# Six columns of attention's output projection run inside attention, with other banks and low parts around the scan and the FFN entries

## The chip, the cores and the metric

The kernel runs on one core of a Trainium2 chip. The metric is the device time of one execution in microseconds (us): the median of the runs.

## The reference

One step of a two-layer streaming encoder on 1024 prompt rows and 64 sample rows, D = 1024, all in float32. Layer 0 is a Mamba-2 scan with a SwiGLU FFN, layer 1 a banded attention with another.

```python
# layer 0
zxbcdt = rmsnorm(x) @ ssm_w_in          # z, x|B|C, dt
xbc = silu(conv4(x|B|C));  dt = softplus(dt + bias)
y, state = ssd_scan(xbc, dt, -exp(A_log), B, C, h0)    # chunks of 64, 32 heads of 64, 4 groups, state 128
y = rmsnorm_per_group((y + xs * D) * silu(z)) @ ssm_w_out
x = x + rmsnorm(y)
x = x + rmsnorm((silu(u @ w_g) * (u @ w_u)) @ w_out)   # u = rmsnorm(x); hidden 2816
# layer 1: K, V from x; q from rmsnorm(x); 16 heads of 64, 9 chunks of 64 keys, clipped relative bias
x = x + rmsnorm(band_attention(q, K, V) @ attn_w_o)
x = x + FFN(x)                                          # as above
```

## The kernel before

Everything is held transposed, features on the 128 partitions and rows on the free axis. The 1088 rows are cut in three slices `SL` (384, 384, 320) for the scan and attention, and in four quarters `QS` (256, 256, 288, 288) for the projections and FFNs. A float32 product is made of three passes: a matrix is split in a rounded high part and a low part (value minus high part), and `passes` issues high x high, high x low, low x high for each of the 8 blocks of 128 features. `unit` takes a PSUM bank, calls `passes` (24 matmuls) and evacuates the result. The third of each three matmuls is the only reader of a weight's low part.

`Weights` streams the weights through rings: SyncE loads one 128 x 1024 tile into a `raw` buffer, `part` casts it on ScalarE into a slot of the ring `hl` (or `hx`), and VectorE subtracts for the low part (line 341). For a weight planned with `acc` the low part is made otherwise: ScalarE writes the negated high part (335), and a DMA issued by GpSimd (336) loads the weight again from DRAM and adds it. A plan lists all weights in the order of use; a slot is taken again when the weight in it is given back with `W.put`. In the FFN's later part two weights are combined into sums (`pair`: ta, tb, half) for a Strassen scheme: `run_pair`. The first `NB0` = 6 hidden blocks run as plain products (`plain_pairs`, results in tiles `x`, PSUM tiles `mmx`), each with a gate and a mult weight, while VectorE and ScalarE build the sums of the activations (`op_build`, lines 1141 to 1174) that the first `run_pair` (tiles `px`) needs. `NACC` = 3 of the six are loaded with `acc`.

A `Stream` sets the order of the program: each `unit` advances a clock by the planned length of its matmuls, and side tasks (generators: norms, scan steps, attention blocks) are woken by that clock with waits from tables such as `TB_V`. Each engine then runs its own instructions in that order, with few exceptions where a priority is raised.

In the scan, `table_task` makes the running sum of the decay (`acsp`, copied to `nac`, line 696), `ssd_task` transposes (`xtp`, 866), multiplies (`xd`, `xe`) and makes states (`sp`, 885) and outputs (`yp`, 816). The norm's sums (`nst`, 487) and its broadcast (`nbp`, 517) take banks from `ax`: the pool `pax` has two banks, shared with xtp and sp; `pyy` has four, for yp.

In attention, heads go in pairs j = 0 to 7. `att_task` makes scores (S, 1681), transposes (ptp, 1712) and po (1747); a pair's result goes to DRAM (`oscr`) and `build_o` loads it back as split tiles `r`, with the last pair taken from SBUF. `uo[q]` is set when quarter q has all of them. Three columns (m = 0, 1, 2) of quarter 0's output projection run before attention's end; the rest in `start_att` by `project`, by groups `MGS` of weights.

Of the kernel before, what the change touches and what calls it, by code (L numbers as in the profile page):

```python
# [46 lines left out]
ST_W, ST_RB = (6.5, 22.0, 22.0), (6.0, 1.0, 1.0)  # L47
TB_W, TB_V = 1.0, 14.0
ES = 0.5, 0.5, 0.0
# [325 lines left out]
def hybrid_kernel(  # L375
# [57 lines left out]
    def col(c):  # L433
        return pcs[:, c:c + 1]

    def ax(name):
        return pax.tile([P, 512], F32, tag="ax", name=name)

# [129 lines left out]
    W.plan(*[dict(src=[w_in[t]]) for t in (32, 36, 16)])  # L568
    for grp in order:
        W.plan(*[dict(src=[w_in[{"B": 32, "C": 36, "x": 16, "z": 0}[kd_] + i]]) for kd_, i in grp])  # L570

# [31 lines left out]

    def project(qs, uq, y, src, after=None, early=None, pl=None):


        ss = {}
        for mg in MGS:
            ws = early if early and mg is MGS[0] else [W.get() for _ in mg]
            for q in qs:  # L610
                n = QS[q][1]
                st.wait_for(lambda: q in uq)
                for m, w_ in zip(mg, ws):
                    ym = y[q][m // 4][:, m % 4, :]

                    def ev(ps):
                        with tc.high_priority(HIP):
                            if src is None:
                                A.copy(ym, ps[:, :n])
                            else:  # L620
                                V.tensor_tensor(ym, src[q][m // 4][:, m % 4, :], ps[:, :n], op=ALU.add)

                    if not (ws is early and q == qs[0]):
                        unit(w_, uq[q], n, ev, pl=pl)
                    if after:
                        if m == 0:
                            ss[q] = ssum_start(n)
                        add_sq(ss[q], ym, n, m == 0)
                    if q == qs[-1]:
                        W.put()  # L630
# [7 lines left out]
    with ExitStack() as es:  # L638
# [413 lines left out]
        for s in range(NSL):  # L1052
# [24 lines left out]
            pend[s] = [dps] * (s < 2) + box  # L1077
        finish(2)
        for grp in order:
            ws = [W.get() for _ in grp]  # L1080
# [27 lines left out]
        project((0, 1), uy[0], ya, None)  # L1108
        st.wait_for(lambda: so["D"] == 3 * XT and len(rst_done) == NG * NSL)


# [116 lines left out]
    def ffn_plan(layer):  # L1228
        w1, w2 = w_f1[layer], w_f2[layer]
        W.plan(*[dict(src=[w1[i]], acc=t_ < NACC) for t_ in range(NB0) for i in (t_, FT + t_)])  # L1230
        for t_ in [*range(NB0, FT), *range(NB0)]:
# [8 lines left out]
    def plain_pairs(ts, ops, hd, px, tmp):  # L1240

        n = ops.n
        ws = [(W.get(), W.get()) for t_ in ts]
        for q in range(2):
            st.wait_for(lambda: all(a_ in ops.plain for a_ in (f"a{q + 1}1", f"a{q + 1}2")))
            uq = ops.plain[f"a{q + 1}1"] + ops.plain[f"a{q + 1}2"]
            for t_, w2 in zip(ts, ws):
                x = tmp.tile([P, n], F32, tag=("p1", "u3")[q] + f"{t_ % 2}", name="x")

                def gate(ps):  # L1250
                    with tc.high_priority(HIP):
                        A.activation(x, ps[:, :n], AF.Silu)

                def mult(ps):
                    with tc.high_priority(HIP):
                        V.tensor_tensor(x, ps[:, :n], x, op=ALU.mult)
                    nc.sync.dma_start(hd[:, t_, q * n:(q + 1) * n], x)

                for w, e in zip(w2, (gate, mult)):
                    unit(w, uq, n, e, pl=px)  # L1260
                    if q:
                        W.put()

# [270 lines left out]
    for j in range(2, 8):  # L1534
        W.plan(W_K[j], W_V[j], W_Q[j])
    for b in range(2):
        W.plan(*[dict(src=[w_o[m]]) for mg in MGS for m in mg])
    ffn_plan(1)
    done = done2
    uo = {}  # L1540
    with ExitStack() as es:
# [230 lines left out]
        def build_o():  # L1772

            for q, (o, n) in enumerate(QS):
                got = []
                of = ((0,), (0, 1), (1, 2), (2,))[q]
                for kh in range(2):
# [8 lines left out]
                    got += [(h[:, k, :], l_[:, k, :]) for k in range(4)]  # L1786
                if nk == 3:
                    yield 0, 0, lambda: all((7, s) in att_done for s in of)
                    for s in of:
                        a, b = max(o, SL[s][0]), min(o + n, SL[s][0] + SL[s][1])  # L1790
                        src = last_o[s][:, a - SL[s][0]:b - SL[s][0]]
                        with tc.high_priority(HIP):
                            A.copy(h[:, 3, a - o:b - o], src)
                            V.tensor_tensor(l_[:, 3, a - o:b - o], src, h[:, 3, a - o:b - o], op=ALU.subtract)
                uo[q] = got

# [77 lines left out]

        st.wait_for(lambda: 0 in uo and R.free())
        y0 = v4(R.get(), QS[0][1])
        wo = [W.get() for _ in MGS[0]]
        for m, w in enumerate(wo):
            unit(w, uo[0], QS[0][1], lambda p_: A.copy(y0[:, m, :], p_[:, :QS[0][1]]), parts=4)
        st.wait_for(lambda: cur["C"] == 8 * NCH and 1 in uo)  # L1880
# [4 lines left out]
    def start_att(ops, px, after, dn):  # L1885
        st.wait_for(lambda: RX.free(4))
        y = ops[0].y
        for q in range(2):
            y[q] = [v4(RX.get(), QS[q][1]) for _ in range(2)]
        G.tensor_copy(y[0][0][:, :3, :], y0[:, :3, :])  # L1890
        project((0, 1), uo, y, None, lambda q, ss: after(q, y[q], ss), early=wo, pl=px)
        R.put()
        st.spawn(op_build(ops[0], dn))
# [106 lines left out]
```

## Time and profile before

| what | before |
|---|---|
| median of 3 runs | 2969.83 us (2967.94 to 2970.08) |
| profiled execution | 2970.8 us, span 2969.1 us |
| mean granted TensorE clock | 0.996 |
| busy: PE, DVE, ACT, POOL | 2916.9, 2037.2, 1394.6, 723.7 us |
| HBM read, written | 292.47, 62.74 MB |

The profile is of one execution. Its times are in us from the span's start. A group's row ends in its busy time, the mean of one in ns, and the idle time of its engine just before it with the instruction that ended most of that. PE is TensorE, DVE VectorE, ACT ScalarE, POOL GpSimd, SP SyncE. Instruction rows of the timeline give start, length, engine, line, operation, tiles and, in brackets, idle time before it and who ended it.

### The profile page before, as it was taken

To read this page: it belongs to the slowest core of one execution; us is meant where nothing else is said; L and a number is where in the kernel's file an instruction comes from. 1 tells how busy PE (TensorE), PEld (TensorE's weight loads), DVE (VectorE), ACT (ScalarE), POOL (GpSimd) and SP (SyncE) were. 2 spreads that over 40 slices of the span, in tenths; PEclk is the share of its full clock that TensorE was granted. 3 is DMA by queue.
4 is the path that set the end of the run, shared out by engine and by line. 5 is a ranking of instruction groups with operands and counts; after the bars stand their busy time and mean duration, and the time that the engine had idled before them with its cause. 6 is when DMAs were issued, how large, how long until landed. Compare 5 with 4: busy or idle time off the path is not lost.

```text
span 2969.1 us, 56218 instructions
## 1 busy us (share of the span) xinstructions
PE 2916.9 (98%) x21562; PEld 2871.9 (97%) x21562; DVE 2037.2 (69%) x4455; ACT 1394.6 (47%) x2522; POOL 723.7 (24%) x877
## 2 busy tenths in 40 slices
PE   8999999999999999999999999999999999999999
PEld 7899999999999999999999899999899999999999
DVE  7887888785768555584557878778678645475544
ACT  6564645454454222244545666556653322244443
POOL 1333333331121343451111000000131333351111
PEclk9999999999999999999999999999999999999999
DMA  3333323234564222255655322223365222245654
GB/s 123 113 106 96 104 90 110 93 118 150 172 172 129 79 76 84 73 161 175 208 175 169 96 75 78 66 67 99 110 186 171 79 79 77 78 156 171 220 174 137
DMA packets 201550, 363.35 MB, mean 122 GB/s; under 512 B 20544, under 2 KB 149280, under 8 KB 201280
## 3 DMA queue, kind: packets, MB, share of 16 engines
q1 hardware_dynamic: 199488, 353.39, 38.3%
q0 software_dynamic: 1792, 6.36, 1.1%
q8 instruction: 169, 2.77, 0.4%
q14 instruction: 101, 0.83, 0.1%
HBM read 292.47 MB, written 62.74 MB: 120 GB/s over the span
## 4 chain that ended last, share of the span: by engine, by line
PE 85%; DVE 8%; DMA 3%; ACT 2%; issue 2%; POOL 0%; SPq 0%; DVEq 0%; ACTq 0%; POOLq 0%
PE px L1280 9%; PE px L1281 9%; PE px L1282 9%; PE mm L454 7%; PE mm L456 7%; PE mm L455 7%; PE po L1480 6%; PE po L1481 6%; PE po L1479 6%; PE mmx L455 3%; PE mmx L454 3%; PE mmx L456 3%; PE ptp L1712 2%; PE po L1747 2%; PE yp L816 1%
## 5 line engine op out<-in xcount | busy, mean ns | idle before, releaser
L454 PE MATMUL mm<-r,hl 128*128 128x384 f32 (+2 forms) x1664 | 555.1, 334 | 6.1 <-ACT BT L768 3.0
L456 PE MATMUL mm<-r,hl 128*128 128x384 f32 (+2 forms) x1664 | 539.6, 324 | 3.6 <-DVE hl L353 2.9
L455 PE MATMUL mm<-r,hl 128*128 128x384 f32 (+2 forms) x1664 | 538.2, 323 | 0.0
L341 DVE TENSOR_TENSOR hl<-raw,hl 128x1024 fp32r<-128x1024 f32 (+1 forms) x219 | 257.2, 1175 | 226.8 <-ACT hl L340 220.7
L1281 PE MATMUL px<-r,hl 128*128 128x288 f32 (+1 forms) x1184 | 347.3, 293 | 0.0
L454 PEld LDWEIGHTS mm<-r,hl 128*128 128x128 f32 x1664 | 315.4, 190 | 9.0 <-ACT BT L768 3.2
L456 PEld LDWEIGHTS mm<-r,hl 128*128 128x128 f32 x1664 | 314.5, 189 | 5.7 <-DVE hl L353 4.5
L455 PEld LDWEIGHTS mm<-r,hl 128*128 128x128 f32 x1664 | 315.3, 190 | 0.3
L1280 PE MATMUL px<-r,hl 128*128 128x288 f32 x1056 | 311.0, 294 | 0.0
L1282 PE MATMUL px<-r,hl 128*128 128x288 f32 x1056 | 310.7, 294 | 0.0
L340 ACT CAST hl<-raw 128x1024 fp32r<-128x1024 f32 (+1 forms) x219 | 220.0, 1005 | 175.3 <-PE po L1481 101.6
L480 POOL TENSOR_TENSOR ssum<-ssum,sq 128x256 f32<-128x256 f32 (+3 forms) x97 | 127.8, 1318 | 637.3 <-ACT sq L479 622.0
L1281 PEld LDWEIGHTS px<-r,hl 128*128 128x128 f32 x1184 | 222.3, 188 | 0.0
L1282 PE MATMUL px<-rx,hl 128*128 128x256 f32 x768 | 214.8, 280 | 6.7 <-DVE hl L341 6.7
L1280 PE MATMUL px<-rx,hl 128*128 128x256 f32 x768 | 215.3, 280 | 0.7 <-ACT hl L340 0.7
L1480 PE MATMUL po<-rx,hl 128*128 128x384 f32 (+1 forms) x624 | 201.7, 323 | 0.1
L1280 PEld LDWEIGHTS px<-r,hl 128*128 128x128 f32 x1056 | 198.4, 188 | 0.4 <-DVE u L1295 0.3
L1282 PEld LDWEIGHTS px<-r,hl 128*128 128x128 f32 x1056 | 198.3, 188 | 0.0
L1479 PE MATMUL po<-rx,hl 128*128 128x384 f32 (+1 forms) x608 | 197.3, 324 | 0.0
L1481 PE MATMUL po<-rx,hl 128*128 128x384 f32 (+1 forms) x608 | 196.5, 323 | 0.0
L1281 PE MATMUL px<-rx,hl 128*128 128x256 f32 x640 | 178.7, 279 | 0.0
L290 POOL TENSOR_TENSOR tt<-raw 128x512 f32<-128x512 f32 x40 | 54.7, 1367 | 438.6 <-DMA raw<-in_w_f_dram 308.9
(360 smaller groups left out, 8053.6 us busy)
## 6 DMA issues: line engine op xcount, KB each, us to landing
raw<-in_w_f_dram SPq DMA_DIRECT2D x154, 512.0 KB, 3.8
rx<-in_w_f_dram SPq DMA_DIRECT2D x54, 512.0 KB, 3.6
raw<-in_w_in_dram SPq DMA_DIRECT2D x40, 512.0 KB, 3.6
MT<-ascr SPq DMA_DIRECT2D x48, 384.0 KB, 4.3
sg<-hscr SPq DMA_DIRECT2D x88, 192.0 KB, 3.5
raw<-in_w_f_dram SPq DMA_DIRECT2D x44, 384.0 KB, 3.2
raw<-in_w_so_dram SPq DMA_DIRECT2D x32, 512.0 KB, 3.8
raw<-in_w_kv_dram SPq DMA_DIRECT2D x18, 512.0 KB, 3.5
```

The costliest lines, as they stand in the source:

```text
L340: self.nc.scalar.copy(h, v)
L341: (eng or self.eng or self.nc.vector).tensor_tensor(lo, v, h, op=ALU.subtract)
L454: PE.matmul(ps[:, :n], h_, xh, start=(first and i == 0), stop=False)
L455: PE.matmul(ps[:, :n], h_, xl, start=False, stop=False)
L456: PE.matmul(ps[:, :n], l_, xh, start=False, stop=(last and i == nk - 1))
L480: (eng or G).tensor_tensor(ssum[:, :n], ssum[:, :n], q[:, :n], op=ALU.add)
L1280: PE.matmul(ps, wh, ah[:, k, :], start=(k == 0), stop=False)
L1281: PE.matmul(ps, wh, al[:, k, :], start=False, stop=False)
L1282: PE.matmul(ps, wl, ah[:, k, :], start=False, stop=(k == 3))
L1479: PE.matmul(ps[:, :n], wh, xh, start=(k == 0), stop=False)
L1480: PE.matmul(ps[:, :n], wh, xl, start=False, stop=False)
L1481: PE.matmul(ps[:, :n], wl, xh, start=False, stop=(k == FT - 1))
```

## The change

- `TB_V` is 10 instead of 14. The first group of the scan's weights after the initial three (x1, z0) is planned with `acc`.
- While the scan's order loop runs, `nst` and `nbp` take their banks from `pyy`.
- The last plain block of each FFN (t = 5) is planned with `acc`, and from the second block on the four units of a block run as gate on quarter 0, gate on quarter 1, mult on 0, mult on 1, not gate, mult, gate, mult.
- At attention's end six columns of quarter 0 run instead of three. Columns 0 and 1 are begun without the last pair of heads (`part_o`, 21 matmuls each) and finished when it is there. Columns 3 and 4 of quarter 1 are begun likewise and finished in `project`, which now starts with group (3, 4, 5) for quarter 1, then (0, 1, 2) for quarter 1, and then (6, 7) for both. Weights 0 to 2 of the projection are loaded a second time.

```diff
@@ constants
-TB_W, TB_V = 1.0, 14.0
+TB_W, TB_V = 1.0, 10.0
@@ -433,7 +433,11 @@
     def col(c):
         return pcs[:, c:c + 1]
 
+    side = [None]
+
     def ax(name):
+        if side[0] and name in ("nst", "nbp"):
+            return side[0].tile([P, 512], F32, tag="yy", name=name)
         return pax.tile([P, 512], F32, tag="ax", name=name)
 
     def mm(name):
@@ the scan's weights
-    for grp in order:
-        W.plan(*[dict(src=[w_in[{"B": 32, "C": 36, "x": 16, "z": 0}[kd_] + i]]) for kd_, i in grp])
+    for g_, grp in enumerate(order):
+        W.plan(*[dict(src=[w_in[{"B": 32, "C": 36, "x": 16, "z": 0}[kd_] + i]], acc=g_ < 1) for kd_, i in grp])
@@ -601,13 +605,25 @@
                 yield 0.5, 0
             uy[half][q] = got
 
-    def project(qs, uq, y, src, after=None, early=None, pl=None):
+    def project(qs, uq, y, src, after=None, early=None, pl=None, begun=None):
 
 
         ss = {}
-        for mg in MGS:
-            ws = early if early and mg is MGS[0] else [W.get() for _ in mg]
-            for q in qs:
+
+        def square(q, ym, n):
+            first = q not in ss
+            if first:
+                ss[q] = ssum_start(n)
+            add_sq(ss[q], ym, n, first)
+
+        groups = [(mg, qs, None) for mg in MGS]
+        if early:
+            for m in MGS[0] + MGS[1]:
+                square(qs[0], y[qs[0]][m // 4][:, m % 4, :], QS[qs[0]][1])
+            groups = [(MGS[1], qs[1:], early), (MGS[0], qs[1:], None), (MGS[2], qs, None)]
+        for mg, gq, ws in groups:
+            ws = ws or [W.get() for _ in mg]
+            for q in gq:
                 n = QS[q][1]
                 st.wait_for(lambda: q in uq)
                 for m, w_ in zip(mg, ws):
@@ -620,13 +636,16 @@
                             else:
                                 V.tensor_tensor(ym, src[q][m // 4][:, m % 4, :], ps[:, :n], op=ALU.add)
 
-                    if not (ws is early and q == qs[0]):
+                    if (q, m) in (begun or {}):
+                        ps_ = begun.pop((q, m))
+                        passes(ps_, w_, lambda k: uq[q][k], [(KD - 1, KD - 1)], n, first=False)
+                        ev(ps_)
+                        st.pump()
+                    else:
                         unit(w_, uq[q], n, ev, pl=pl)
                     if after:
-                        if m == 0:
-                            ss[q] = ssum_start(n)
-                        add_sq(ss[q], ym, n, m == 0)
-                    if q == qs[-1]:
+                        square(q, ym, n)
+                    if q == gq[-1]:
                         W.put()
                 if mg is MGS[-1]:
                     R.put(4)
@@ before the order loop
 finish(2)
+        side[0] = pyy
...
@@ after the last project of the scan
+        side[0] = None
@@ ffn_plan
-        W.plan(*[dict(src=[w1[i]], acc=t_ < NACC) for t_ in range(NB0) for i in (t_, FT + t_)])
+        W.plan(*[dict(src=[w1[i]], acc=t_ < NACC or t_ == NB0 - 1) for t_ in range(NB0) for i in (t_, FT + t_)])
@@ -1240,26 +1261,29 @@
     def plain_pairs(ts, ops, hd, px, tmp):
 
         n = ops.n
-        ws = [(W.get(), W.get()) for t_ in ts]
-        for q in range(2):
+        first = ts == PGS[0]
+        xs, ws = {}, {}
+        for t_, i, q in [(t_, i, q) for t_ in ts for i, q in (((0, 0), (1, 0), (0, 1), (1, 1)) if first else ((0, 0), (0, 1), (1, 0), (1, 1)))]:
+            if (t_, i) not in ws:
+                ws[t_, i] = W.get()
             st.wait_for(lambda: all(a_ in ops.plain for a_ in (f"a{q + 1}1", f"a{q + 1}2")))
             uq = ops.plain[f"a{q + 1}1"] + ops.plain[f"a{q + 1}2"]
-            for t_, w2 in zip(ts, ws):
-                x = tmp.tile([P, n], F32, tag=("p1", "u3")[q] + f"{t_ % 2}", name="x")
-
-                def gate(ps):
-                    with tc.high_priority(HIP):
-                        A.activation(x, ps[:, :n], AF.Silu)
-
-                def mult(ps):
-                    with tc.high_priority(HIP):
-                        V.tensor_tensor(x, ps[:, :n], x, op=ALU.mult)
-                    nc.sync.dma_start(hd[:, t_, q * n:(q + 1) * n], x)
-
-                for w, e in zip(w2, (gate, mult)):
-                    unit(w, uq, n, e, pl=px)
-                    if q:
-                        W.put()
+            if i == 0:
+                xs[t_, q] = tmp.tile([P, n], F32, tag=("p1", "u3")[q] + f"{t_ % 2}", name="x")
+            x = xs[t_, q]
+
+            def gate(ps):
+                with tc.high_priority(HIP):
+                    A.activation(x, ps[:, :n], AF.Silu)
+
+            def mult(ps):
+                with tc.high_priority(HIP):
+                    V.tensor_tensor(x, ps[:, :n], x, op=ALU.mult)
+                nc.sync.dma_start(hd[:, t_, q * n:(q + 1) * n], x)
+
+            unit(ws[t_, i], uq, n, mult if i else gate, pl=px)
+            if q:
+                W.put()
 
     def run_pair(t_, pr, bs, ends, ops, hd, px, tmp, apart=False):
 
@@ attention's plan of weights
-    for b in range(2):
-        W.plan(*[dict(src=[w_o[m]]) for mg in MGS for m in mg])
+    for mg in MGS[:2] + MGS[:1] + MGS[2:] + MGS:
+        W.plan(*[dict(src=[w_o[m]]) for m in mg])
-    uo = {}
+    uo, part_o = {}, {}
@@ build_o
+                    part_o[q] = got
...
+                    yield 0, 2.5 if q < 2 else 0
@@ -1872,11 +1898,34 @@
                     if s == 0:
                         st.spawn(build_o())
 
-        st.wait_for(lambda: 0 in uo and R.free())
-        y0 = v4(R.get(), QS[0][1])
-        wo = [W.get() for _ in MGS[0]]
-        for m, w in enumerate(wo):
-            unit(w, uo[0], QS[0][1], lambda p_: A.copy(y0[:, m, :], p_[:, :QS[0][1]]), parts=4)
+        st.wait_for(lambda: 0 in part_o and R.free(2))
+        y0 = [v4(R.get(), QS[0][1]) for _ in range(2)]
+        n0, begun = QS[0][1], {}
+        for mg in MGS[:2]:
+            wo = [W.get() for _ in mg]
+            for m, w in zip(mg, wo):
+                if m < 2:
+                    begun[m] = mm("mm")
+                    passes(begun[m], w, lambda k: part_o[0][k], [(k, k) for k in range(KD - 1)], n0, parts=4, last=False)
+                    st.pump()
+                    if m == 0:
+                        continue
+                    st.wait_for(lambda: 0 in uo)
+                    for m_ in range(2):
+                        passes(begun[m_], wo[m_], lambda k: uo[0][k], [(KD - 1, KD - 1)], n0, first=False)
+                        A.copy(y0[0][:, m_, :], begun[m_][:, :n0])
+                        W.put()
+                        st.pump()
+                    continue
+                unit(w, uo[0], n0, lambda p_: A.copy(y0[m // 4][:, m % 4, :], p_[:, :n0]), parts=4)
+                if mg is MGS[0]:
+                    W.put()
+        begun.clear()
+        st.wait_for(lambda: 1 in part_o)
+        for m, w in list(zip(MGS[1], wo))[:2]:
+            begun[1, m] = mm("mm")
+            passes(begun[1, m], w, lambda k: part_o[1][k], [(k, k) for k in range(KD - 1)], QS[1][1], parts=4, last=False)
+            st.pump()
         st.wait_for(lambda: cur["C"] == 8 * NCH and 1 in uo)
 
 
@@ -1887,9 +1936,10 @@
         y = ops[0].y
         for q in range(2):
             y[q] = [v4(RX.get(), QS[q][1]) for _ in range(2)]
-        G.tensor_copy(y[0][0][:, :3, :], y0[:, :3, :])
-        project((0, 1), uo, y, None, lambda q, ss: after(q, y[q], ss), early=wo, pl=px)
-        R.put()
+        G.tensor_copy(y[0][0], y0[0])
+        G.tensor_copy(y[0][1][:, :2, :], y0[1][:, :2, :])
+        project((0, 1), uo, y, None, lambda q, ss: after(q, y[q], ss), early=wo, pl=px, begun=begun)
+        R.put(2)
         st.spawn(op_build(ops[0], dn))
         st.wait_for(lambda: 2 in uo and R.free(4))
         y = ops[1].y
```

The number of matmuls is the same. On VectorE in the early scan (the copy `nac` of the running sum, the convolution steps of `CT` and `xsT`, `craw` evacuating a bank), before:

```order
L691 TENSOR_TENSOR tt<-dt,negA 128x288
L761 SCALAR_TENSOR_TENSOR CT<-craw,pcs,CT 128x323
L721 TENSOR_TENSOR craw<-mm,rb_145 128x64
L761 SCALAR_TENSOR_TENSOR CT<-craw,pcs,CT 128x323
L786 COPY Bn<-bnp 128x384
L761 SCALAR_TENSOR_TENSOR xsT<-craw,pcs,xsT 128x323 x3
L721 TENSOR_TENSOR craw<-mm,rb_143 128x384
L792 TENSOR_TENSOR CB<-cbp,U 128x384
L761 SCALAR_TENSOR_TENSOR xsT<-craw,pcs,xsT 128x384 x3
L696 COPY nac<-acsp 128x288
L721 TENSOR_TENSOR craw<-mm,rb_144 128x384
```

and now:

```order
L710 TENSOR_TENSOR tt<-dt,negA 128x288
L341 TENSOR_TENSOR hl<-raw,hl 128x1024
L715 COPY nac<-acsp 128x288
L780 SCALAR_TENSOR_TENSOR CT<-craw,pcs,CT 128x323
L780 SCALAR_TENSOR_TENSOR xsT<-craw,pcs,xsT 128x323
L780 SCALAR_TENSOR_TENSOR CT<-craw,pcs,CT 128x323
L780 SCALAR_TENSOR_TENSOR xsT<-craw,pcs,xsT 128x323
L780 SCALAR_TENSOR_TENSOR CT<-craw,pcs,CT 128x323
L780 SCALAR_TENSOR_TENSOR xsT<-craw,pcs,xsT 128x323
L730 TENSOR_TENSOR dec<-nac,lastp 128x288
L805 COPY Bn<-bnp 128x384
```

The copy of acsp has moved from behind the convolution steps of CT and xsT, two evacuations and CB to ahead of CT and xsT.

On VectorE at the first FFN's entry (L308 and L309 make the pair's sums `tt`; L341 with `hl<-raw` is a weight's low part and with `hl<-tt` that of a sum; the `r<-r` rows split activations; `x<-mmx` is a plain block's result), before:

```order
L341 TENSOR_TENSOR hl<-raw,hl 128x1024
L1256 TENSOR_TENSOR x<-mmx,x 128x256
L1154 TENSOR_TENSOR r<-r 128x1152
L341 TENSOR_TENSOR hl<-raw,hl 128x1024
L1154 TENSOR_TENSOR r<-r 128x1152
L308 TENSOR_TENSOR tt<-tt,raw 128x512
L1154 TENSOR_TENSOR r<-r 128x1152
L309 TENSOR_TENSOR tt<-raw,tt 128x512
L1256 TENSOR_TENSOR x<-mmx,x 128x256
L1154 TENSOR_TENSOR r<-r 128x1152 x2
L341 TENSOR_TENSOR hl<-tt,hl 128x1024
```

and now:

```order
L308 TENSOR_TENSOR tt<-tt,raw 128x512
L1281 TENSOR_TENSOR x<-mmx,x 128x256
L309 TENSOR_TENSOR tt<-raw,tt 128x512
L341 TENSOR_TENSOR hl<-raw,hl 128x1024
L1175 TENSOR_TENSOR r<-r 128x1152 x4
L341 TENSOR_TENSOR hl<-tt,hl 128x1024
L1281 TENSOR_TENSOR x<-mmx,x 128x256
L1175 TENSOR_TENSOR r<-r 128x1152
```

Of the two low parts from `raw` only one is left, behind both steps of the sums, and the two steps of the sums stand together.

On TensorE at attention's end (po and ptp of the last blocks, `mm` columns of the output projection inside attention, `mmx` those after it), before:

```order
L1682 MATMUL S<-K_23899,Ql_24582 128x128
L1747 MATMUL po<-pT,Vn 64x128 x10
L1712 MATMUL ptp<-ident,sc 128x128 x10
L1747 MATMUL po<-pT,Vn 64x128 x10
L1712 MATMUL ptp<-ident,sc 128x128 x10
L1747 MATMUL po<-pT,Cv 64x64 x8
L1747 MATMUL po<-pT,Vn 64x64 x2
L454 MATMUL mmx<-r,hl 128x256
L455 MATMUL mmx<-r,hl 128x256
L456 MATMUL mmx<-r,hl 128x256
```

and now, with 55 more rows of `mm` ahead of the first one shown:

```order
L459 MATMUL mm<-r,hl 128x256
L460 MATMUL mm<-r,hl 128x256
L1736 MATMUL ptp<-ident,sc 128x128 x10
L458 MATMUL mm<-r,hl 128x256
L459 MATMUL mm<-r,hl 128x256
L460 MATMUL mm<-r,hl 128x256
L1771 MATMUL po<-pT,Cv 64x64 x8
L1771 MATMUL po<-pT,Vn 64x64 x2
L458 MATMUL mm<-r,hl 128x256
```

Between the last transposes and the first `mmx` stood only po; now matmuls of the projection stand on both sides of the transposes and of po.

## The prediction

> **What bounds the kernel now.** I read the page's engine shares first, then the chain that ended last, then TensorE's waits, and last the windows around the places that the change touches.
>
> ```profile
> span 2969.1 us, 56218 instructions
> ...
> PE 2916.9 (98%) x21562; PEld 2871.9 (97%) x21562; DVE 2037.2 (69%) x4455; ACT 1394.6 (47%) x2522; POOL 723.7 (24%) x877
> ...
> PE 85%; DVE 8%; DMA 3%; ACT 2%; issue 2%; POOL 0%; SPq 0%; DVEq 0%; ACTq 0%; POOLq 0%
> ```
>
> TensorE (PE) is busy for 2916.9 of 2969.1 us and is 85% of the chain. The change leaves its matmuls as many and as wide as they were, so it can only win from the 52 us in which PE is idle and from stretches at a lower clock. Where those 52 us lie is told by PE's waits (total, times, longest, in us):
>
> ```profile
> PE px L1282 <- DVE hl L341: 6.7, 3, 2.6
> PE xtp L866 <- DVE nv L498: 4.8, 6, 0.8
> PE sp L885 <- POOL xe L877: 3.9, 1, 3.9
> PE mm L454 <- ACT BT L768: 3.0, 1, 3.0
> PE nst L487 <- DVE nv L499: 3.0, 2, 2.7
> PE S L1681 <- DVE pT L1716: 2.9, 5, 0.9
> ...
> PE sp L885 <- DVE xd L876: 1.2, 1, 1.2
> ...
> PE nbp L517 <- DVE nv L498: 0.8, 1, 0.8
> PE sp L885 <- ACT rb L520: 0.8, 1, 0.8
> ...
> PE nbp L517 <- DVE hn L898: 0.7, 1, 0.7
> ...
> PE px L1280 <- ACT hl L340: 0.7, 1, 0.7
> ```
>
> They fall into the change's five places. The px rows are the entry of the two FFNs (three long waits, 2.6 the longest). The xtp, nst, nbp and the 0.8 sp row are waits for a PSUM bank inside the scan. The BT, xe and xd rows are the early scan. The S row is attention. The windows show the clock (the last column but two) and how full PE and DVE are there; columns are PE, PEld, DVE, ACT, POOL, then PEclk, DMA share, GB/s:
>
> ```profile
> 71.10:74.50 3.40, 3.40 (x13) 3.31 (x12) 2.27 (x7) 1.72 (x5) 0.63 (x2) 0.50 0.52 157
> ...
> 101.80:108.60 6.80, 5.59 (x37) 4.75 (x36) 5.76 (x16) 2.00 (x3) 1.79 (x2) 0.50 0.01 3
> ...
> 671.80:675.20 3.40, 3.05 (x15) 3.05 (x16) 3.40 (x19) 1.46 (x5) 0.00 (x0) 0.51 0.53 170
> ...
> 938.10:941.50 3.40, 1.35 (x10) 0.95 (x8) 3.30 (x3) 2.51 (x4) 0.00 (x0) 1.00 0.78 225
> 941.50:944.90 3.40, 2.89 (x13) 2.89 (x14) 2.94 (x4) 2.48 (x3) 2.38 (x2) 0.50 0.21 72
> 2288.30:2291.70 3.40, 0.79 (x7) 0.75 (x7) 3.40 (x4) 0.38 (x1) 0.27 (x1) 1.00 0.58 175
> 2295.00:2298.40 3.40, 1.23 (x10) 1.03 (x10) 3.40 (x5) 0.28 (x1) 0.75 (x1) 1.00 0.00 0
> ```
>
> Behind four of the idle places PE ran at half clock for some 3.4 us (twice that at 101.8). The two waits of layer 1's FFN entry left no such stretch. In both of those DVE is busy for all of 3.40 us: it is DVE's queue that is late.
>
> **Part A: the early scan.** The running sum of the decay (acsp) goes ahead of 36 matmuls, two weights get their low part by an accumulating transfer, and one group of transposes (xtp) stands 36 matmuls earlier. The rows are PE's wait, ACT's cast of the first of the two weights, and DVE's copy of acsp:
>
> ```profile
> 70.74 0.41 PE L454 MATMUL mm<-r,hl 128*128 128x384 f32 x1 [2.99 <-ACT BT L768]
> ```
> ```profile
> 60.54 1.05 ACT L340 CAST hl<-raw 128x1024 fp32r<-128x1024 f32 x1 [1.85 <-PE mmp L456]
> ```
> ```profile
> 80.34 0.46 DVE L696 COPY nac<-acsp 128x288 f32<-128x288 f32 x1
> ```
>
> What an accumulated low part costs is shown by the twelve that the kernel has already (the negated copy on ACT, the issue on POOL, and us from issue to landing; their cast is as long as the one at 60.54), beside the DVE subtraction that it replaces:
>
> ```profile
> L335 ACT ACTIVATE hl<-hl 128x1024 fp32r<-128x1024 f32 x3 | 3.1, 1045 | 0.0
> ...
> L336 POOL DMA_DIRECT2D hl<-in_w_f_dram x3 | 2.6, 869 | 0.9 <-ACT hl L335 0.9
> ```
> ```profile
> DMA to landing us min/median/max: 6.2/8.7/10.4
> ```
> ```profile
> L341 DVE TENSOR_TENSOR hl<-raw,hl 128x1024 fp32r<-128x1024 f32 (+1 forms) x219 | 257.2, 1175 | 226.8 <-ACT hl L340 220.7
> ```
>
> The cast ends at 61.6, one step of BT now stands on ACT between it and the copy, so I put the issue at about 63.4 and the landing 6.2, 8.7 or 10.4 later: 69.6, 72.1 or 73.8. It is read by the third matmul, some 0.5 after the one at 70.74. So the 2.99 wait for the bank gets a companion, 0.9 longer at the median, 2.6 at worst. On the other side DVE loses 2 x 1.17 = 2.3 from its queue ahead of the bank's reader and of dt, and the acsp copy moves from 80.3 to about 76, where DVE now waits for it with the steps of CT and xsT behind it. The waits of sp (3.9 and 1.2) may shrink by up to what those transposes gain, but the multiplications xd and xe behind them still go through DVE and POOL one after the other. I follow the queue to the first yp at 105.9 and find the same time within what I can tell: 0, from -3 (most of the two sp waits less the late low part) to +3.
>
> The Trainium skill, "DMA: Bandwidth & Descriptors", section "Anatomy of one DMA — SWDGE (gpsimd) path", fits a transfer issued by GpSimd as 2.0 us plus its bytes over 436e3. By that, 512 KB would land after an estimated 3.2 us, no low part of this change would ever be late, and the sum below would be 2.1 lower. The trace disagrees for the accumulating kind: its least is 6.2, and I use the trace.
>
> **Part B: the scan's banks.** nst and nbp leave the ring of two banks that they share with xtp and sp for the ring of four that yp uses.
>
> ```profile
> 242.35 0.49 PE L487 MATMUL nst<-ident,ssg 128*128 128x128 f32 x3
> 243.64 0.52 PE L866 MATMUL xtp<-ident,xsT 128*128 128x128 f32 x3 [0.80 <-DVE nv L498]
> 243.91 0.42 PE L454 MATMUL mm<-r,hl 128*128 128x384 f32 x1
> ```
> ```profile
> 670.21 0.47 DVE L933 TENSOR_TENSOR ssg<-ssg,sq 128x320 f32<-128x320 f32 x1
> ```
>
> xtp reads nothing of nv; it waits until DVE has reduced nst out of its bank. The matmuls behind it (243.91) need no DVE result, so nothing else holds PE there: six times 0.8, the row's 4.8, go. The three single bank waits (0.8, 0.8, 0.7) go likewise, 2.3, of which I take 1.7, since DVE is full around the last of them. Of the long nst wait at 668 (2.7) nothing goes: its input ssg is itself ready only at 670.68, with DVE full. Sum -6.5; bounds -9 (DVE's reduction no longer urgent, ssg earlier, and half of the half-clock stretch at 671.8) and -4 (only the six, each keeping 0.1).
>
> **Part C: FFN entry, layer 0.** Two DVE subtractions (2.3) leave DVE's queue ahead of the parts of the first pair, and gate and mult weights of a plain pair now come free evenly, the gate weight after two quarters instead of three. The waits of 0.7 (the px row of ACT's cast) and 1.90 go:
>
> ```profile
> 942.01 0.58 PE L1282 MATMUL px<-rx,hl 128*128 128x256 f32 x1 [1.90 <-DVE hl L341]
> ```
>
> With them goes, I think, the half-clock stretch: PE did there 2.89 of work at half speed, 1.4 lost. New is the pair of accumulated low parts for the last plain pair. Their slots come free one whole pair ahead, 96 matmuls. The attention-end row of part D has 174 in 20.00, 0.115 each, so 11.0 ahead. Cast, copy and semaphores take 2.3; 8.7 remain for a landing of 6.2 to 10.4. Spread evenly that is a wait of 0.3 each on average and 1.7 at most. -0.7 -1.9 -1.4 +0.6 = -3.4, taken as -3 since DVE's own order is tight; from -4.3 (no stretch, all in time) to +1 (both late by 1.7, the waits staying in part).
>
> The half-clock stretch begins at 941.5, right after 3.40 us in which PE was still busy for 1.35. The Trainium skill, "TensorE: Matmul & The Clock Gate", section "Part 1: The HAM clock gate", has the clock halve after an idle window of about 3.4 us. By that strictly, a window with 1.35 of work is no idle one, the stretch does not come from these waits, and the sum would be 1.4 higher; the trace speaks for the waits, and I take the 1.4.
>
> **Part D: attention's end.** Six columns of the first quarter (144 matmuls) and 48 matmuls of the second stand inside attention or right at its end, where three columns (72) stood: 120 more.
>
> ```profile
> 2080.00:2084.00 4.00, 2.60 (x17) 2.13 (x16) 3.05 (x6) 2.90 (x6) 0.00 (x0) 1.00 0.59 166
> 2084.00:2130.00 46.00, 43.26 (x393) 39.12 (x392) 35.39 (x105) 27.18 (x59) 1.46 (x5) 1.00 0.19 56
> ...
> 2130.00:2150.00 20.00, 20.00 (x174) 20.00 (x174) 7.24 (x7) 13.21 (x25) 7.42 (x8) 1.00 0.66 222
> ```
> ```profile
> raw<-in_w_o_dram SPq DMA_DIRECT2D x12, 512.0 KB, 3.6
> ```
>
> The 120 take 13.8 and are done either way; inside attention they can only fill its idle time. Of that, 4.00 - 2.60 = 1.4 lies before the first column stands in the order, and 46.00 - 43.26 = 2.7 remain: attention ends 11.1 later, and 13.8 less is left behind it. I take -3 with the small idle time around the next norm. Against it stand three weights loaded a second time: 3 x 512 KB, three casts (1.05) and three subtractions (1.2), 3.5 on a DVE that is busy for 7.24 of 20. POOL's bigger copies of finished columns lie beside PE as long as q1's columns cover them. Bounds -4.4 and +6 (rival 1).
>
> **Part E: FFN entry, layer 1.** The same edit as C meets waits of 2.6 (the longest of the px row) and 2.17.
>
> ```profile
> 2297.63 0.38 PE L1282 MATMUL px<-rx,hl 128*128 128x256 f32 x1 [2.17 <-DVE hl L341]
> ```
> ```profile
> 2288.42 1.35 DVE L1154 TENSOR_TENSOR r<-r 128x1152 fp32r<-128x1152 f32 x1
> 2289.69 1.21 DVE L341 TENSOR_TENSOR hl<-tt,hl 128x1024 fp32r<-128x1024 f32 x1
> ```
>
> Ahead of that L341 DVE now has 2.3 less, and one of the 1.35 splits stands behind it: 3.7, more than the 2.6. The second part then also moves forward. -4.8 + 0.6 = -4.2, taken as -3.5 because DVE stays full (3.40 of 3.40) there; from -4.8 to +1.
>
> **Sum.** 0 - 6.5 - 3 - 3 - 3.5 = -16. The profiled execution took 2970.8 (span 2969.1 and 1.7 around it), 1.0 above the median of 2969.83. I make the sum against it: 2954.8. The upper ends (+3, +2.5, +4, +9, +4.5 above the values taken) combine as independent to about 11, the lower ones to about 5.
>
> **Rivals.** (1) *Weights run short at attention's end.* The reloaded columns serve one quarter only, 24 matmuls or 2.8 each, while a weight that was not fetched ahead takes 3.6 + 1.05 + 1.2 = 5.9. If none is fetched ahead, 3 x (5.9 - 2.8) = +9.2: 2964.0. For it: the DMA moves 222 GB/s there already. Against it: SP's order puts the first reloads before attention's last writes. 10%.
>
> (2) *Slower: accumulated low parts come late.* All of them are used about when they land. If the POOL queue (its issue waits for ACT's copy, with the pair's sums behind it) adds 2 us to the longest landing, 12.5, then each of the four FFN weights holds PE for 12.5 - 8.7 = 3.8, with a half-clock stretch of 1.4 behind each: 20.8; the first scan weight holds it 4.7. Less the 2.1 in the sum (0.9 in A, 1.2 in C and E), +23.4: 2978. It decides from landings of about 11. For it: 10.4 occurs. Against it: eleven of twelve are below that. 9%.
>
> (3) *The scan's bank waits only move.* If DVE's answers behind xtp (xd) hold PE a few matmuls later, B is 0: 2961.3. For it: DVE is the releaser in all those rows. Against it: the matmuls at 243.91. 14%.
>
> (4) *More half-clock stretches go.* With those at 71.1 and 101.8 (3.40 and 5.59 of work, 1.7 and 2.8 lost) and at 671.8 (1.5) gone too: -6.0, 2948.8. For it: each follows a wait that the change touches. Against it: those waits stay in part. 10%.
>
> **How the numbers follow.** The forecast has the remaining 57%. A measurement here can tell about 0.2%, 6 us, from no change, so faster means below 2963.9. Nearly all of the forecast's share, and (3) and (4), are faster: 0.77. (1) and the forecast's upper tail are within: 0.13. (2) and a tail of it: 0.10. The range from 2946 to 2968 holds (1), (3), (4) and the forecast with its combined ends, and leaves out (2) and tails of about 10%.
>
> **What would show it.** Right: PE's row xtp <- nv gone; both px rows of the FFN entries below 0.5; no half clock at the first FFN entry; attention's window with under 2 us idle; w_o's reloads cast before their columns. Wrong: a px or mmx row released by the DMA of w_f (low parts late), a mmx row released by w_o's weights, or sp and mm rows in the first 110 us longer in sum than 8.

## The result, and the profile after

| | before | changed |
|---|---|---|
| median | 2969.57 us (2967.94 to 2970.08, 4 runs) | 2949.24 us (2947.48 to 2953.14, 4 runs) |
| profiled execution | 2970.8, span 2969.1 | 2953.1, span 2951.4 |

The ratio is 0.9934 [0.9917, 0.9951]: 20.3 us less by the medians, 17.7 by the two profiled executions (the changed one is the slowest of its four). The forecast was 2954.8, 16 less. The total was close; the terms were not.

The page's span and shares, then TensorE's waits of the changed kernel (total, times, longest):

```profile
span 2951.4 us, 56260 instructions
...
PE 2911.9 (99%) x21562; PEld 2871.3 (97%) x21562; DVE 2032.0 (69%) x4452; ACT 1402.8 (48%) x2531; POOL 728.2 (25%) x884
```
```profile
PE px L1306 <- DVE hl L341: 5.2, 3, 1.9
PE nbp L521 <- DVE y L849: 3.0, 1, 3.0
...
PE S L1705 <- DVE pT L1740: 2.6, 4, 1.1
...
PE px L1304 <- DVE x L1281: 1.7, 1, 1.7
...
PE xtp L885 <- ACT zs L967: 1.4, 1, 1.4
PE mmx L460 <- DVE hl L341: 1.1, 1, 1.1
...
PE mm L460 <- DMA hl<-in_w_in_dram: 0.6, 1, 0.6
...
PE sp L904 <- DVE hn L917: 0.6, 1, 0.6
```

Gone are the six xtp waits (4.8), the bank's 3.0 at BT and sp's 3.9. The px row of the FFN entries, which should have gone, is 5.2 against 6.7, and the largest new rows are 3.0 at nbp and 1.7 at px. Where the time went is read best from the start of the same matmul in both traces (counted by tile name; dtn is the one that opens the decay's tables):

| matmul | before | changed | difference | part that lies ahead of it |
|---|---|---|---|---|
| first dtn | 55.03 | 53.72 | -1.3 | none |
| first yp | 105.94 | 96.82 | -9.1 | A |
| last sp | 653.13 | 636.40 | -16.7 | B |
| first mmx | 714.31 | 696.31 | -18.0 | B |
| first px | 937.43 | 919.54 | -17.9 | C's plain blocks |
| 200th px | 967.09 | 950.09 | -17.0 | C |
| 400th ptp | 2001.26 | 1985.74 | -15.5 | none |
| last mmx | 2286.49 | 2268.50 | -18.0 | D |
| last po | 2955.99 | 2938.00 | -18.0 | E |

So 1.3 is there before any edit (the first dtn stands between 53.0 and 55.6 in the fourteen profiles of this case), A gave 7.8 where the sum had 0, B 8.9 where it had 6.5, C cost 1.0 where it had -3, D gave 2.5 (3 in the sum), E nothing where it had -3.5. Between the 200th px and the 400th ptp 1.5 was given back, in places that the change does not touch. Nearly all of it (1.4) is a stretch of half clock that the changed kernel has at 1663.8. Both traces have the same wait of 2.20 just ahead of that place, and only one has the stretch behind it. The windows behind that wait, before first (columns as in the prediction):

```profile
1680.90:1684.30 3.40, 3.40 (x22) 3.13 (x23) 2.50 (x7) 1.61 (x5) 0.00 (x0) 1.00 0.28 53
```
```profile
1663.80:1667.20 3.40, 3.40 (x14) 3.30 (x15) 2.37 (x7) 0.97 (x4) 0.00 (x0) 0.50 0.25 51
```

The windows by stage, the three rows of before first:

```profile
0.00:112.00 112.00, 95.31 (x566) 89.73 (x567) 85.19 (x211) 66.68 (x118) 14.32 (x51) 0.92 0.36 111
112.00:600.00 488.00, 482.34 (x3418) 471.44 (x3417) 407.25 (x1036) 257.72 (x396) 186.77 (x302) 1.00 0.33 103
600.00:720.00 120.00, 114.78 (x886) 112.53 (x885) 85.17 (x210) 59.91 (x111) 24.32 (x32) 0.99 0.38 119
```
```profile
0.00:112.00 112.00, 101.07 (x621) 95.54 (x622) 89.99 (x230) 74.84 (x130) 20.09 (x60) 0.97 0.45 137
112.00:600.00 488.00, 487.32 (x3467) 478.26 (x3466) 409.39 (x1049) 262.85 (x403) 187.67 (x302) 1.00 0.32 102
600.00:720.00 120.00, 115.74 (x920) 113.58 (x919) 88.06 (x207) 58.66 (x117) 22.53 (x28) 0.99 0.45 140
```

In the first 112 us PE is idle for 10.9 instead of 16.7, and the granted clock is 0.97 instead of 0.92: less idle time and less half clock together. In the scan's body PE's idle time falls from 5.7 to 0.7.

### The profile page after: what moved, and what is told of

Same layout as the page of the kernel before. It is cut to its first block, busy times and chain, and to the rows that moved or that the text cites. A ratio compares the mean times of both kernels' runs of the same rounds, so it can differ in the third digit from the quotient of the medians.

```text
span 2951.4 us, 56260 instructions
## 1 busy us (share of the span) xinstructions
PE 2911.9 (99%) x21562; PEld 2871.3 (97%) x21562; DVE 2032.0 (69%) x4452; ACT 1402.8 (48%) x2531; POOL 728.2 (25%) x884
## 4 chain that ended last, share of the span: by engine, by line
PE 86%; DVE 7%; DMA 3%; ACT 2%; issue 1%; POOL 0%; SPq 0%; DVEq 0%; ACTq 0%; POOLq 0%
PE px L1304 9%; PE px L1305 9%; PE px L1306 9%; PE mm L458 7%; PE mm L460 7%; PE mm L459 7%; PE po L1504 6%; PE po L1505 6%; PE po L1503 6%; PE mmx L460 3%; PE mmx L459 3%; PE mmx L458 3%; PE ptp L1736 2%; PE po L1771 2%; PE S L1705 1%
## 5 line engine op out<-in xcount | busy, mean ns | idle before, releaser
L458 PE MATMUL mm<-r,hl 128*128 128x384 f32 (+2 forms) x1704 | 565.5, 332 | 3.2 <-DVE craw L740 1.0
L460 PE MATMUL mm<-r,hl 128*128 128x384 f32 (+2 forms) x1704 | 549.9, 323 | 4.3 <-DVE hl L353 2.9
L459 PE MATMUL mm<-r,hl 128*128 128x384 f32 (+2 forms) x1704 | 548.5, 322 | 0.0
L341 DVE TENSOR_TENSOR hl<-raw,hl 128x1024 fp32r<-128x1024 f32 x216 | 255.6, 1184 | 217.8 <-ACT hl L340 215.6
L458 PEld LDWEIGHTS mm<-r,hl 128*128 128x128 f32 x1704 | 322.2, 189 | 6.0 <-DVE craw L740 1.1
L460 PEld LDWEIGHTS mm<-r,hl 128*128 128x128 f32 x1704 | 321.5, 189 | 6.2 <-DVE hl L353 4.2
L459 PEld LDWEIGHTS mm<-r,hl 128*128 128x128 f32 x1704 | 322.2, 189 | 0.3
L340 ACT CAST hl<-raw 128x1024 fp32r<-128x1024 f32 x216 | 216.9, 1004 | 161.5 <-PE po L1505 102.3
L1306 PEld LDWEIGHTS px<-rx,hl 128*128 128x128 f32 x768 | 145.3, 189 | 5.9 <-DVE hl L341 5.9
```

Source lines behind the costliest of these rows:

```text
L340: self.nc.scalar.copy(h, v)
L341: (eng or self.eng or self.nc.vector).tensor_tensor(lo, v, h, op=ALU.subtract)
L458: PE.matmul(ps[:, :n], h_, xh, start=(first and i == 0), stop=False)
L459: PE.matmul(ps[:, :n], h_, xl, start=False, stop=False)
L460: PE.matmul(ps[:, :n], l_, xh, start=False, stop=(last and i == nk - 1))
L1306: PE.matmul(ps, wl, ah[:, k, :], start=False, stop=(k == 3))
```

## The experiments

Each kernel is the changed one with one edit, but for b_only, which is the one before with one edit. Their runs were timed beside runs of the kernel before. With intervals of some 4 us on each ratio, a difference of less than about 5 us between two kernels is not settled by the medians; there I read the traces.

The traces can be compared more finely than the medians, by the time between the same two matmuls in all fourteen profiles. Profiles with half of a part are on neither side; for B, i_side_off and i_nst_only count as with it; for D the two f_only kernels are left out.

| part | from, to | without it, us | with it, us |
|---|---|---|---|
| A | first dtn, first yp | 50.3 to 50.9 (3 profiles) | 42.0 to 43.6 (9) |
| B | first yp, first mmx | 608.1 to 608.4 (2) | 597.1 to 599.5 (12) |
| C | first mmx, 200th px | 252.8 to 254.0 (3) | 252.8 to 254.8 (9) |
| D | 400th ptp, last mmx | 285.1 to 285.2 (3) | 282.0 to 283.9 (9) |
| E | last mmx, last po | 669.2 to 669.5 (3) | 668.8 to 669.5 (9) |

So A is worth 7 to 9, B 9 to 11, D 1 to 3, and C and E nothing within 2. The medians of all runs:

| kernel | median, us | ratio to before [95%] |
|---|---|---|
| changed | 2949.24 | 0.9934 [0.9917, 0.9951] |
| u_scan_start | 2959.37 | 0.9966 [0.9953, 0.9978] |
| a_only_order | 2952.41 | 0.9940 [0.9927, 0.9952] |
| a_only_low | 2956.22 | 0.9955 [0.9941, 0.9968] |
| i_low_two | 2953.26 | 0.9949 [0.9934, 0.9963] |
| u_banks | 2963.03 | 0.9973 [0.9964, 0.9983] |
| b_only | 2960.16 | 0.9965 [0.9952, 0.9979] |
| i_side_off | 2954.11 | 0.9948 [0.9934, 0.9963] |
| i_nst_only | 2949.46 | 0.9933 [0.9920, 0.9946] |
| u_ffn_entry | 2950.89 | 0.9936 [0.9924, 0.9949] |
| f_only_low | 2952.36 | 0.9941 [0.9928, 0.9953] |
| f_only_order | 2954.87 | 0.9949 [0.9937, 0.9962] |
| u_att_end | 2953.61 | 0.9948 [0.9935, 0.9962] |

**The early scan undone, u_scan_start.**

```diff
-TB_W, TB_V = 1.0, 10.0
+TB_W, TB_V = 1.0, 14.0
...
-... acc=g_ < 1)])
+... acc=g_ < 0)])
```

> The changed kernel with part A undone: TB_V is 14 again and x1 and z0 get their low parts from VectorE. Theory from the two traces (the early scan gave most): about 8 us slower than the changed kernel, some 12 faster than before. The prediction's sum (part A is worth 0): the same as the changed kernel, 20 faster than before.

10.1 slower than the changed kernel, and the two intervals do not overlap. Part A is worth about 10 by the medians and 7.8 by the two traces, from the first dtn to the first yp; the prediction's 0 falls. Its waits of TensorE are those of before:

```profile
PE sp L904 <- POOL xe L896: 3.9, 1, 3.9
...
PE mm L458 <- ACT BT L787: 3.0, 1, 3.0
...
PE sp L904 <- DVE xd L895: 1.3, 1, 1.3
```

**Its two halves, a_only_order** (`acc` taken away, TB_V 10) **and a_only_low** (TB_V 14, `acc` kept).

> The changed kernel with the low parts of x1 and z0 from VectorE again; TB_V stays 10, so acsp and xtp stay early. Theory: the wait of 3.0 at the bank (67 us) is VectorE's queue, so it returns with a half-clock stretch of 1.7, while the wait of 3.9 at sp stays gone: some 4 us slower than the changed kernel. Rival: the order alone does it (VectorE's order changed too) and the low parts are worth nothing: the same as the changed kernel.

> The changed kernel with TB_V 14 again; x1 and z0 keep the accumulated low parts. Theory: the bank's wait at 67 us stays short, sp's 3.9 and 1.2 and the half-clock stretch behind them return: some 5 us slower than the changed kernel. Rival (order alone): 8 to 10 us slower, as with the whole part undone.

3.2 and 7.0 slower than the changed kernel; together the 10.1. Neither is clear of the intervals, and from the first dtn to the first yp the two take only 2.2 and 3.8 longer, 6.0 of the 7.8. But on the waits the traces are plain. Without the accumulated low parts (a_only_order) the bank's wait is back, sp's is not:

```profile
PE mm L458 <- ACT BT L787: 3.0, 1, 3.0
...
PE sp L904 <- DVE hn L917: 0.6, 1, 0.6
```

Without the early running sum (a_only_low) it is the other way round:

```profile
PE sp L904 <- POOL xe L896: 4.0, 1, 4.0
...
PE mm L460 <- DMA hl<-in_w_in_dram: 0.5, 1, 0.5
```

Each half removes its own wait, as the theory had it; the rival that the order alone does it falls.

**More of the same, i_low_two** (`acc=g_ < 2`).

> The changed kernel with accumulated low parts for the scan's second group (x2, z1) as well. Theory (what helped in the early scan is VectorE's queue): VectorE loses 2.3 more between 80 and 100 us; the waits of 1.4 and 0.5 there shrink: 0 to 2 us faster than the changed kernel, and if the low parts land late, a PE row released by the DMA of w_in shows it. Rival (only what stands ahead of 70 us counts): the same.

Not faster (4 slower, within the intervals; from the first dtn to the first yp it takes 42.8, the changed kernel 43.1, so the 4 is not lost there). Its trace has new waits in the place of the old ones:

```profile
PE sp L904 <- POOL xe L896: 2.1, 1, 2.1
PE mm L458 <- DVE craw L740: 1.8, 2, 1.2
PE mm L460 <- DMA hl<-in_w_in_dram: 1.3, 1, 1.3
```

The theory that a shorter VectorE queue helps anywhere in the early scan falls; it helped where a low part stood ahead of the reader of a bank. Why sp waits longer here stays open.

**The banks undone, u_banks** (the line `side[0] = pyy` taken out), **and the banks alone, b_only** (`side` put into the kernel before).

> The changed kernel with part B undone: nst and nbp take their banks from the ring of two again. Theory from the traces and the prediction's part B agree: 6 to 7.5 us slower than the changed kernel, 13 faster than before; the xtp waits of 0.8 are back. Rival (3), the waits only move: the same as the changed kernel.

> The kernel before with part B alone: in the scan's order loop and the projection behind it nst and nbp take their banks from the ring of four. The prediction's part B: 6.5 us faster than before. Theory from the traces (six waits of 0.8, the waits at the scan's end traded for one of 3.0, and the half-clock stretches changed): 7 to 9 faster, no xtp row among PE's waits, one nbp row of 3.0. If the difference between the medians with part B undone (13.8) is B's true worth and not luck with half-clock stretches: 12 or more faster.

u_banks is 13.8 slower than the changed kernel, b_only 10.6 faster than before: -6.2 to -14.3 by its interval. Part B is worth some 10, over the 6.5 of the prediction; its rival (3), that the waits only move, falls for the six xtp waits, and holds for the waits at the scan's end. The first row is of u_banks, the second of b_only, which has no xtp row:

```profile
PE xtp L885 <- DVE nv L502: 4.8, 6, 0.8
```
```profile
PE nbp L521 <- DVE y L834: 3.0, 1, 3.0
```

**Which of the two tiles, and where: i_side_off** (`side[0] = None` ahead of the projection behind the loop) **and i_nst_only** (`name == "nst"`).

> The changed kernel, with nst and nbp back in the ring of two from the end of the scan's order loop on; inside the loop they keep the ring of four. Theory (the new wait of 3.0 at nbp comes from the ring of four, whose bank holds a yp that VectorE reads late): the wait and its half-clock stretch go, those of before (0.7, 2.7, 0.8) come back: within 2 us of the changed kernel, and of part B's worth the six xtp waits are nearly all. Rival (the ring of four is what the scan's end needs): 4 or more slower.

> The changed kernel with nst alone in the ring of four; nbp stays in the ring of two throughout. Theory: the wait of 3.0 at nbp goes, and so do the xtp waits, since it is nst's bank that xtp waited for: 1 to 4 us faster than the changed kernel. Rival (VectorE is late there and whatever comes next waits as long): the same, with the 3 us at another row.

i_side_off keeps the 3.0: that nbp is issued inside the loop, so my theory of where it stands was wrong, and the edit only brought two small waits back (0.7 and 0.6). The 4.9 by which it is slower is not in its trace (its profiled execution was its fastest run, 2951.6) and stays open. i_nst_only takes the 3.0 away and the xtp waits too, and is as fast as the changed kernel, 2949.46. Its trace shows the time at other rows, as the rival said:

```profile
PE sp L904 <- ACT rb L524: 1.1, 1, 1.1
...
PE nst L491 <- DVE ssg L952: 1.0, 1, 1.0
PE nst L491 <- DVE y L849: 0.9, 1, 0.9
PE nbp L521 <- DVE hn L917: 0.7, 1, 0.7
```

At the scan's end VectorE is late; the bank only says which row waits for it.

**The FFN entries undone, u_ffn_entry** (both edits), **and each alone: f_only_low** (`first = True`, so the old order) **and f_only_order** (`acc=t_ < NACC`).

> The changed kernel with parts C and E undone: the low parts of the last plain block from VectorE, and gate, mult, gate, mult in both FFNs. Theory from the traces (waits only changed place at the FFN entries): within 1.5 us of the changed kernel, either way. The prediction's sum (C and E worth 6.5): 6.5 slower than the changed kernel, 14 faster than before.

> The changed kernel with gate, mult, gate, mult in the plain blocks again; the last block keeps its accumulated low parts. Theory from the traces (the new order puts two VectorE evacuations last, so the first pair's second quarter waits for its bank): the wait of 1.7 for the bank goes; a wait for a low part that is needed 2.8 earlier comes, 0 to 2 in each layer: within 2 us of the changed kernel. Rival (order and low parts are only good together): 3 or more slower.

> The changed kernel with the last block's low parts from VectorE; the new order of the units stays. Theory: VectorE's 2.3 are back ahead of the pair's parts, the waits at the FFN entries grow by up to that in each layer: 2 to 4 us slower than the changed kernel. Rival: the subtractions fall into VectorE's idle time before the pair's sums and cost nothing: the same.

1.7, 3.1 and 5.6 slower than the changed kernel by the medians; none is outside the intervals. For parts C and E together the medians rule out little more than a loss above 6 or a gain above 7, so the prediction's 6.5 falls by the table of stretches and not by them. How the two edits hang together is in the traces. With the low parts alone, the mult weight is needed one unit after the gate weight, and its low part comes late in both layers (first row). With the order alone, VectorE's low parts are late for the plain block itself, in the first layer (2.1 of the mmx row; the other 1.0 is at attention's end and in the changed kernel too), and for the pair (two rows of f_only_order):

```profile
PE mmx L460 <- DMA hl<-in_w_f_dram: 7.0, 2, 3.7
```
```profile
PE px L1306 <- DVE hl L341: 5.0, 3, 2.9
PE mmx L460 <- DVE hl L341: 3.1, 2, 2.1
```

From the first mmx to the 200th px and from the 400th ptp to the last po, f_only_order takes 3.4 and 2.2 longer than the changed kernel, f_only_low 0.1 and 0.5: its 7.0 stand in the place of waits at px, of which 0.7 are left. So each edit makes a wait that the other takes away, and the two together stand about where the kernel stood without them.

**Attention's end undone, u_att_end.**

```diff
-    for mg in MGS[:2] + MGS[:1] + MGS[2:] + MGS:
-        W.plan(*[dict(src=[w_o[m]]) for m in mg])
+    for b in range(2):
+        W.plan(*[dict(src=[w_o[m]]) for mg in MGS for m in mg])
...
-        st.wait_for(lambda: 0 in part_o and R.free(2))
+        st.wait_for(lambda: 0 in uo and R.free())
...
+        for m, w in enumerate(wo):
+            unit(w, uo[0], QS[0][1], lambda p_: A.copy(y0[:, m, :], p_[:, :QS[0][1]]), parts=4)
```

> The changed kernel with part D undone: three columns inside attention, as before. Theory from the traces and the prediction agree: 2.5 to 3 us slower than the changed kernel, some 17 faster than before. Rival (1), weights run short: the same or faster than the changed kernel.

4.4 slower by the medians, within the intervals, and in the direction and size of the 2.5 that the table of matmuls shows. From the 400th ptp to the last mmx u_att_end takes 285.1, before 285.2, the changed kernel 282.8.

## Why the prediction held, and where it did not

**Part A failed in its size.** Three steps of it were wrong. The rows are POOL's issue of the first low part, VectorE's evacuation, and TensorE's waits, all of the changed kernel:

```profile
62.08 0.90 POOL L336 DMA_DIRECT2D hl<-in_w_in_dram  x1 [1.93 <-ACT hl L335]
```
```profile
64.58 0.22 DVE L740 TENSOR_TENSOR craw<-mm,rb 128x64 f32<-128x64 f32 x1
```
```profile
67.43 0.44 PE L460 MATMUL mm<-r,hl 128*128 128x384 f32 x1 [0.65 <-DMA hl<-in_w_in_dram]
...
94.90 0.52 PE L885 MATMUL xtp<-ident,xsT 128*128 128x128 f32 x3 [1.42 <-ACT zs L967]
95.99 0.91 PE L904 MATMUL sp<-xe,Bn 128*128 128x128 f32 x6 [0.57 <-DVE hn L917]
```

First, the low part landed 5.3 after its issue, under the least of the twelve (6.2): PE went on at 67.43, not 72.1. (Its issue at 62.08, not 63.4, is the 1.3 that was there before any edit: from the cast to the issue it took 2.9, as in the sum.) Second, "the 2.99 wait for the bank gets a companion" was wrong. In before, three subtractions of 1.2 stood in VectorE's queue (62.22, 65.39, 68.87) ahead of the evacuation at 70.38 that PE waited for; in the changed kernel two are gone and the third stands behind it, the evacuation ends at 64.80, and the wait is gone. I had the 2.3 in the text and did not carry them to the bank. Third, I let the gain of sp's waits end in the chain of xd and xe; but the first group's xtp, 36 matmuls earlier, has its xd and xe done while other matmuls run, and 5.1 of waiting became 2.0. a_only_order and a_only_low show the second and the third apart. Between the first dtn and the first yp the waits fell from 8.1 to 3.0; the rest of the 7.8 is the clock, 0.97 for 0.92 in the window of 112 us. The clock differs between runs of one kernel too (u_banks: 0.995 to 0.998 in its nine runs of 2958.6 to 2965.2), but the 7.8 repeats to about 1 in the nine profiles with part A.

**Part B held in its mechanism and was too small.** Counted between the same matmuls of b_only and before, each wait of 0.8 that goes is worth 0.96, and the first xtp of each three, which shows no wait in either trace, 0.24: 6.5 for nine transposes instead of 4.8. A wait of 0.4 at 328 also went, worth 0.5. And "Of the long nst wait at 668 (2.7) nothing goes" was wrong in part: that wait went (2.9), but VectorE's lateness came out ten us earlier as the nbp wait of 3.0, so it nearly cancels. The rows show the first xtp of the six places, now without a wait, and the new wait, with the VectorE work that it waits for:

```profile
234.29 0.49 PE L885 MATMUL xtp<-ident,xsT 128*128 128x128 f32 x3
```
```profile
645.62 0.60 DVE L849 SCALAR_TENSOR_TENSOR y<-xsT,pcs,yp 128x384 f32<-128x384 f32 x1
```
```profile
646.28 0.43 PE L521 MATMUL nbp<-ident,rst 128*128 128x128 f32 x2 [3.02 <-DVE y L849]
```

**Parts C and E failed in the same step.** I asked whether the accumulated low parts would be in time, and they were: the plain blocks have no wait for them. I did not ask enough what is late next. The rows are VectorE's and TensorE's at the first FFN's entry:

```profile
914.80 5.15 DVE L1175 TENSOR_TENSOR r<-r 128x1152 fp32r<-128x1152 f32 x4
...
926.57 0.42 DVE L1281 TENSOR_TENSOR x<-mmx,x 128x256 f32<-128x256 f32 x1
...
928.17 1.22 DVE L341 TENSOR_TENSOR hl<-tt,hl 128x1024 fp32r<-128x1024 f32 x1
```
```profile
927.13 0.36 PE L1304 MATMUL px<-rx,hl 128*128 128x256 f32 x1 [1.72 <-DVE x L1281]
929.44 0.39 PE L1306 MATMUL px<-rx,hl 128*128 128x256 f32 x1 [1.84 <-DVE hl L341]
```

The first part (ta) was ready in time, as I had it. But the same four splits still stand in VectorE's queue (5.15), the second part (tb) is late by as much as the first was before, and the last block's two mult results, which the new order puts last, are evacuated behind the splits too, so a bank is late (1.72). What had left VectorE's queue (2.3 in each layer) came back for the most part as waiting, 4.1 more in both layers together. The cast and the negated copy of an accumulated low part take 2.1 of ScalarE's queue, here just ahead of the norm's broadcast `rb`, and VectorE waits for `rb` (the first row is of the changed kernel, the second of u_ffn_entry):

```profile
DVE r L1246 <- ACT rb L524: 5.8, 3, 2.6
```
```profile
DVE r L1246 <- ACT rb L524: 1.7, 1, 1.7
```

f_only_low, which has these low parts, has 3.8 of this wait; f_only_order, which has not, has none. I had counted ScalarE's copies as time before the landing, and not for what stands behind them on ScalarE. Nor did the half-clock stretch go; it now stands right behind the two waits:

```profile
929.60:933.00 3.40, 3.40 (x18) 3.40 (x19) 3.13 (x6) 0.42 (x1) 1.16 (x1) 0.55 0.30 87
```

The Trainium skill, "TensorE: Matmul & The Clock Gate", section "Part 1: The HAM clock gate", asks for an idle window of about 3.4 us. Here waits of 1.72 and 1.84 with some matmuls between them were followed by a stretch, as 0.7 and 1.9 were in before, so the trace speaks against a window that must be wholly idle. But the two rows at 1680.9 and 1663.8 show that the same wait is followed by a stretch in one trace and not in the other, so the 1.4 that the sum of part C took for the stretch was not tied to these waits alone. In layer 1 the waits are 1.9 and 1.5 for 2.6 and 2.2, with 0.8 new: 4.2 for 4.8.

**Part D held.** Attention's window and the one behind it, after:

```profile
2069.00:2124.00 55.00, 54.38 (x501) 52.10 (x500) 38.82 (x106) 31.08 (x66) 2.62 (x6) 1.00 0.24 76
2124.00:2144.00 20.00, 18.94 (x160) 18.74 (x159) 11.99 (x9) 15.00 (x30) 12.30 (x13) 1.00 0.91 305
```

0.6 idle where 2.7 were. Behind it the low part of column 6's weight is 1.1 late (VectorE). That weight is the first to be loaded behind the three reloads: rival (1) in small, and the sign that the prediction named, an mmx row released by a weight of w_o. The DMA moves 305 GB/s there, against 222 before, and was not what PE waited for.

**The rivals.** (1) came with 1.1 of its 9.2. (2) did not come: landings in the changed kernel run from 5.3 to 11.1, but the six that the change added took 5.3 to 7.9. (3) is refuted by u_banks and b_only, but for the scan's end. (4) came in part in the first 112 us. That the sum was near is luck: A and B together gave 16.7 for 6.5, C, D and E 1.5 for 9.5.

## What to carry to other kernels

When a step leaves a full queue, carry its time forward to every reader behind it, bank readers too, before calling it nought; and when a wait goes, work out the next late item on that same queue, since a full VectorE only hands the wait on. Work that moves to another engine also has a queue behind it there: ask who waits for that. A wait for a PSUM bank that another tile shares is paid in full and is cheap to take away: give the short-lived tile a ring whose old readers are long done. Two edits that each remove one wait may each make the other's; test them singly.

## What I had not expected of the hardware

A wait of 0.8 cost 0.96 between the same two matmuls, in all six places. Accumulating transfers of 512 KB landed between 5.3 and 11.1 us after their issue in one execution of the changed kernel (the row is of their line):

```profile
DMA to landing us min/median/max: 5.3/8.1/11.1
```

The Trainium skill's fit for transfers issued by GpSimd ("DMA: Bandwidth & Descriptors", "Anatomy of one DMA — SWDGE (gpsimd) path") gives an estimate of 3.2 for this size; no accumulating transfer here came near it. And stretches of half clock come and go where the two kernels are alike: one stands in before at 43.8 (first row) and none in the changed kernel's profile (second row), ahead of every edit. Of the fourteen profiles eight have one there. Half of its 3.40, 1.7, is my estimate of what one costs.

```profile
43.80:47.20 3.40, 3.40 (x14) 3.40 (x13) 2.29 (x5) 2.23 (x4) 0.56 (x3) 0.50 0.02 5
```
```profile
41.00:48.00 7.00, 4.66 (x30) 4.37 (x29) 5.64 (x23) 3.11 (x6) 1.32 (x5) 1.00 0.01 2
```
